# Modulation and expert steps of two 512 KB weight tiles instead of one, in a kernel whose TensorE order is planned ahead

## Chip, core and metric

The kernel runs on one core of a Trainium2 chip. The metric is the device time of one execution in microseconds; the smaller, the better. TensorE (PE in the profile) does the matrix products, VectorE (DVE), ScalarE (ACT) and GpSimd (POOL) the rest, and SyncE (SP) issues nearly all loads.

## What is computed

256 tokens of width 1024 go through two networks in turn. The first is one block: an RWKV-7 mixer run in both directions beside a gated linear attention, then a mixture of 32 experts with two experts per token. The second is two layers of an attention block that also carries 256 context tokens through the first layer and part of the second. Its layers are modulated by vectors that depend on two condition vectors alone (c and c_ctx):

```python
def first_block(x, ...):
    h = rmsnorm(x, ln1_w)
    p = h @ w_in
    mix = concatenate([rwkv7_mixer(p[..., :RWKV_COLS], ...), gla_mixer(p[..., RWKV_COLS:], ...)])
    x = x + mix @ w_out
    x = x + hier_moe(rmsnorm(x, ln2_w), ...)          # 32 experts, 2 per token
    return rmsnorm(x, ln_f_w)

def second_block(x, c, ctx, c_ctx, w_ada, ...):
    for l in range(2):
        ml = split(silu(c) @ w_ada[l] + b_ada[l], 9)       # modulation of the tokens
        mc = split(silu(c_ctx) @ w_ada[l] + b_ada[l], 9)   # modulation of the context
        # ffn, mixer over context and tokens, ffn; the same for the context, but for its last parts
```

All weights are float32. `silu(c) @ w_ada` is a product of two rows with a 1024 x 9216 matrix, so it is nearly all loading; the same holds for the experts, which see at most 32 tokens each in this stage.

## The kernel before

**Weights.** Every large weight comes in tiles of 128 x 1024 float32 (512 KB), which `raw` (L303) loads into one of 8 buffers (13 while the context's feed-forward parts have the pool "room" open). The dense layers split a tile into a high and a low part (L319 on ACT, L320 on DVE or POOL) and multiply with three products (`mm3`, L334 to L336). The modulation (`ada`, L1458) and the experts (`moe`, L1338 for gate and up, L1348 for down) multiply the raw tile directly. Their left operand has 32 columns, so each of a tile's four products goes to another 32 columns of the array; the trace shows a tile as 8 matmul instructions of the form 128*32. A layer's modulation has 72 tiles (144 in all), the experts have 256 tiles of gate and up and 128 of down, in 8 groups of four experts.

**Order.** The order of the instructions on PE and SP is the order in which the program issues them; nothing is reordered afterwards. Two generators issue it in turn, `first()` (mixers, then experts) and `second()` (modulation of both layers, then the context's way through the second network), and `_run` (L1993) picks between them by a model of time. At each `yield` a generator tells what the step cost on PE and how long its next step must wait for results. `raw` keeps a second clock, of when each tile will have arrived: 1.46 us per tile at best, and not before its buffer is free (`arrival`, L290).

One of the two generators counts as the *loading* task. `_run` lets it go ahead of the other when the next tile has, by the model, been there for `slack` us (I call the time by which model time is ahead of the arrival, the *lead*); otherwise the other goes first if it is ready. If only one is ready, it goes, whatever the lead.

- While the mixers run, the modulation is the loading task, slack is 2 us, and after each of its steps it must pause 0.5 us (`pace`). So a mixer step that is ready always comes between two steps of the modulation.
- While the experts run, they are the loading task and the context's feed-forward and mixer parts are the other. Slack is 8 us for the first four groups and 2 us for the rest, pace is 0. Here expert steps follow each other until the lead is below the slack.

**The mixers in the order of the trace.** Projections and gated linear attention (`products`, `shifted`, `gla`), 26 to 148 us; the start of `scoring` (head norms, decay), to 177; the loop over `items` in `scoring` with its steps of 5.2, 1.8 and 2.5 us (L839 to L853), to 259; `invert` (L862), a chain of 62 operations on DVE that runs to about 302, while `solve` (L886) waits and `beside` (L663) and the modulation fill PE; the inverse goes to memory and back (L935, L937); `solve` proper, a chain of small products (L916, L943, L962, L906) and copies (L928, L930), 316 to 373; `rwkv_out` and the output projection, to about 440. The experts' stretch is 462 to 1541 us. From there the context's rest and then the tokens run alone with no step that the change touches.

After every 16 tiles of a modulation (8 for the last), four groups of small DVE operations (L1465 to L1469) turn the sums into columns; after its last tile follow L1476, L1480 and `lam` (L1485).

Of the kernel before, what the change touches and what calls it, by code (L numbers as in the profile page):

```python
# [230 lines left out]
class _Net:  # L231
# [1063 lines left out]
    def moe(self, ch, x, load, loads):  # L1295

        nc = self.nc
        mm, V, A = nc.tensor.matmul, nc.vector, nc.scalar
        self.htok = ch.tile([128, 2, D], "htok")
        self.slot, self.wt = ch.tile([128, 2, 32], "slot"), ch.tile([128, 2, 32], "wt")  # L1300
        with ch.scope("rt") as cr:
            yield from self.route(cr, x)
        loads()
        for g in range(8):
            if g == 4:
                self.slack = 2.0
            s = ch.tile([128, 2, 4, 32], "ms")
            sw = ch.tile([128, 2, 4, 32], "msw")
            e = slice(4 * g, 4 * g + 4)
            for i in range(2):  # L1310
                V.tensor_tensor(s[:, i], self.c("iota")[:, None, :].to_broadcast([128, 4, 32]),
                                self.slot[:, i, e, None].to_broadcast([128, 4, 32]), op=OP.is_equal)
                V.tensor_tensor(sw[:, i], s[:, i], self.wt[:, i, e, None].to_broadcast([128, 4, 32]), op=OP.mult)
            xt = ch.tile([128, KD, 128], "mx")
            for q in range(2):
                b = ch.bank()
                for k in range(4):
                    for i in range(2):
                        kk = q * 4 + k
                        mm(b[:, k * 128:k * 128 + 128], self.htok[:, i, kk * 128:kk * 128 + 128],  # L1320
                           s[:, i].rearrange("p a b -> p (a b)"), start=(i == 0), stop=(i == 1))
                A.copy(xt[:, q * 4:q * 4 + 4].rearrange("p a b -> p (a b)"), b)
            st, ws = ch.tile([128, T], "mst", F32R), ch.tile([128, 1], "mws")
            b = ch.bank()
            for i in range(2):
                nc.tensor.transpose(b[:, i * 128:i * 128 + 128], s[:, i].rearrange("p a b -> p (a b)"), self.ident)
            for i in range(2):
                mm(b[:, T:T + 1], sw[:, i].rearrange("p a b -> p (a b)"), self.ones[:, :1], start=(i == 0), stop=(i == 1))
            V.tensor_copy(st, b[:, :T])
            V.tensor_copy(ws, b[:, T:T + 1])  # L1330
            yield 3.9, 0.6
            bg, bu = ch.bank(), ch.bank()
            for k in range(KD):
                for m, b in enumerate((bg, bu)):
                    for q in range(2):
                        r = load(self.d["moe_gu"][(g * KD + k) * 2 + m][:, q * 1024:q * 1024 + 1024])
                        for j in range(4):
                            mm(b[32 * j:32 * j + 32, q * 256:q * 256 + 256], xt[:, k, 32 * j:32 * j + 32],  # L1338
                               r[:, j * 256:j * 256 + 256], start=(k + q == 0), stop=(k == KD - 1), skip_group_check=True)
                        yield 0.45  # L1340
            ht = yield from self.swiglu_rows(ch, bg, bu, 128)
            bb = [ch.bank(), ch.bank()]
            for k in range(4):
                for n in range(2):
                    for q in range(2):
                        r = load(self.d["moe_dn"][(g * 4 + k) * 2 + n][:, q * 1024:q * 1024 + 1024])
                        for j in range(4):
                            mm(bb[n][32 * j:32 * j + 32, q * 256:q * 256 + 256], ht[:, k, 32 * j:32 * j + 32],  # L1348
                               r[:, j * 256:j * 256 + 256], start=(k + q == 0), stop=(k == 3), skip_group_check=True)
                        yield 0.45  # L1350
            y = [ch.tile([128, 2, 512], t, F32R) for t in ("mx", "myl")]
            for n in range(2):
                A.mul(y[0][:, n], bb[n], ws[:, 0:1])
                V.scalar_tensor_tensor(y[1][:, n], bb[n], ws[:, 0:1], y[0][:, n].bitcast(F32), op0=OP.mult, op1=OP.subtract)
            yield 0.0, 0.7
            for d in range(4):
                b = ch.bank()
                for i in range(2):
                    c = (2 * d + i) * 128
                    for n in range(2):  # L1360
                        mm(b[:, i * T:i * T + T], y[n][:, c // 512, c % 512:c % 512 + 128], st, start=(n == 0), stop=(n == 1))
                o = x[:, 2 * d:2 * d + 2].rearrange("p a b -> p (a b)")
                V.tensor_tensor(o, b, o, op=OP.add)
                yield 0.9
# [78 lines left out]
    def ada(self, ch, l):  # L1443

        nc = self.nc
        w = self.d[f"wada{l}"]
        if l == 0:
            yield 0.0, 5.0
        m2 = [self.cp.tile([128, 72], F32, name=f"mod{l}{m}") for m in range(2)]
        for s in range(5):  # L1450
            b = ch.bank()
            nb = 512 if s < 4 else 256
            for k in range(KD):
                for q in range(nb // 256):
                    m, o = (s * KD + k, q) if s < 4 else (4 * KD + k // 2, k % 2)
                    r = self.raw(w[m][:, o * 1024:o * 1024 + 1024])
                    for j in range(4):
                        nc.tensor.matmul(b[32 * j:32 * j + 32, q * 256:q * 256 + 256], self.cond[:, k],  # L1458
                                         r[:, j * 256:j * 256 + 256], start=(k + q == 0), stop=(k == KD - 1),
                                         skip_group_check=True)  # L1460
                    yield 0.45
            for q in range(nb // 128):
                t = ch.tile([128, 128], "adat", bufs=1)
                u = ch.tile([128, 128], "adau", bufs=1)
                nc.vector.tensor_copy(t, b[:, q * 128:q * 128 + 128])  # L1465
                nc.vector.transpose(u, t)
                c = slice(s * 16 + q * 4, s * 16 + q * 4 + 4)
                for m in range(2):
                    nc.vector.tensor_tensor(m2[m][:, c], u.rearrange("p (b c) -> p b c", c=32)[:, :, m],  # L1469
                                            self.v(f"b_ada{l}")[:, c], op=OP.add)  # L1470
        out = []
        for m in range(2):
            mm = m2[m].rearrange("p (n k) -> p n k", k=KD)
            a = self.cp.tile([128, 3, KD], F32, name=f"nsc{l}{m}")
            for i in range(3):
                nc.vector.scalar_tensor_tensor(a[:, i], mm[:, 3 * i + 1], 1.0, self.v(f"norm_g{l}{i}"),  # L1476
                                               op0=OP.add, op1=OP.mult)
            g = self.cp.tile([128, 3, KD], F32, name=f"gsc{l}{m}")
            for i in range(3):
                nc.vector.tensor_scalar(g[:, i], mm[:, 3 * i + 2], 0.5, None, op0=OP.mult)  # L1480
            out.append(dict(shift=[mm[:, 3 * i] for i in range(3)], scale=[a[:, i] for i in range(3)],
                            gate=[g[:, i] for i in range(3)]))
        return out
# [430 lines left out]
class _Stream:  # L1914
# [14 lines left out]
    def load(self, c):  # L1929
        if c not in self.raw:  # L1930
            o = (c % 2) * 1024
            self.raw[c] = self.net.raw(self.src[c // 2][:, o:o + 1024])
# [244 lines left out]
```

## Time and profile before

| | us |
|---|---|
| median of 3 runs | 2898.14 |
| range of the runs | 2897.85 to 2900.83 |
| the profiled execution: its own time | 2895.48 |
| its span, first to last instruction | 2893.7 |
| PE busy in it | 2763.3 |

The profiled execution is 1.8 us longer than its span, and 2.7 us below the median of the runs. A matmul's end is modelled in the profile, so a busy PE may still have gaps; how long a tile really holds PE is read from the starts of the instructions around it. "PEclk" is the clock granted to TensorE, 1.00 for 2.4 GHz and 0.50 for 1.2 GHz. The window views give for each stretch its length, the busy time of each engine with its number of instructions, PEclk, the share of the DMA engines that was busy and the rate of loading.

### The profile page before, as it was taken

To read this page: it belongs to the slowest core of one execution; us is meant where nothing else is said; L and a number is where in the kernel's file an instruction comes from. 1 tells how busy PE (TensorE), PEld (TensorE's weight loads), DVE (VectorE), ACT (ScalarE), POOL (GpSimd) and SP (SyncE) were. 2 spreads that over 40 slices of the span, in tenths; PEclk is the share of its full clock that TensorE was granted. 3 is DMA by queue.
4 is the path that set the end of the run, shared out by engine and by line. 5 is a ranking of instruction groups with operands and counts; after the bars stand their busy time and mean duration, and the time that the engine had idled before them with its cause. 6 is when DMAs were issued, how large, how long until landed. Compare 5 with 4: busy or idle time off the path is not lost. (4 is left out here: it accounts for less than half of the span.)

```text
span 2893.7 us, 59118 instructions
## 1 busy us (share of the span) xinstructions
PE 2763.3 (95%) x24442; PEld 2442.7 (84%) x24442; DVE 1780.1 (62%) x3517; ACT 1235.5 (43%) x2071; POOL 178.8 (6%) x207
## 2 busy tenths in 40 slices
PE   8998879999999999999997999999999999999999
PEld 6765568898667878888886999889999999899999
DVE  4766456455444655455456667767866767776865
ACT  4331133334243433334344445465544545365553
POOL 0110120000000100000001000100200000101100
PEclk9999979999999999999998999999999999999999
DMA  9857767987888888879794566424555565334563
GB/s 331 304 165 241 251 234 279 318 322 262 279 312 292 276 324 336 334 267 378 282 360 172 174 195 201 139 88 130 169 196 193 183 194 200 112 102 144 168 193 130
DMA packets 190849, 667.73 MB, mean 231 GB/s; under 512 B 28786, under 2 KB 29810, under 8 KB 189938
## 3 DMA queue, kind: packets, MB, share of 16 engines
q1 hardware_dynamic: 180144, 656.04, 65.6%
q10 hardware_dynamic: 10434, 7.90, 0.9%
q8 instruction: 192, 3.15, 0.4%
q14 instruction: 79, 0.65, 0.1%
HBM read 658.05 MB, written 5.80 MB: 229 GB/s over the span
## 5 line engine op out<-in xcount | busy, mean ns | idle before, releaser
L320 DVE TENSOR_TENSOR wlo<-raw,whi 128x1024 fp32r<-128x1024 f32 x625 | 769.6, 1233 | 491.4 <-ACT whi L319 480.1
L319 ACT CAST whi<-raw 128x1024 fp32r<-128x1024 f32 x633 | 663.8, 1050 | 775.9 <-issue 260.6
L334 PE MATMUL bz<-hnhz,whi 128*128 128x256 f32 x1920 | 540.6, 282 | 0.7 <-ACT hnhz L328 0.7
L335 PE MATMUL bz<-hnlz,whi 128*128 128x256 f32 x1920 | 533.4, 278 | 4.1 <-DVE hnlz L329 4.1
L336 PE MATMUL bz<-hnhz,wlo 128*128 128x256 f32 x1920 | 532.9, 278 | 1.9 <-DVE wlo L320 1.9
L334 PE MATMUL bc<-hnhc,whi 128*128 128x256 f32 x1504 | 435.1, 289 | 11.5 <-ACT whi L319 8.6
L336 PE MATMUL bc<-hnhc,wlo 128*128 128x256 f32 x1504 | 422.6, 281 | 6.3 <-DVE wlo L320 6.3
L335 PE MATMUL bc<-hnlc,whi 128*128 128x256 f32 x1504 | 423.1, 281 | 4.0 <-DVE hnlc L329 2.2
L334 PEld LDWEIGHTS bz<-hnhz,whi 128*128 128x128 f32 x1920 | 362.4, 189 | 9.6 <-issue 5.7
L335 PEld LDWEIGHTS bz<-hnlz,whi 128*128 128x128 f32 x1920 | 362.4, 189 | 5.5 <-DVE hnlz L329 5.4
L336 PEld LDWEIGHTS bz<-hnhz,wlo 128*128 128x128 f32 x1920 | 362.1, 189 | 2.1 <-DVE wlo L320 2.1
L334 PEld LDWEIGHTS bc<-hnhc,whi 128*128 128x128 f32 x1504 | 287.9, 191 | 51.6 <-issue 32.3
L336 PEld LDWEIGHTS bc<-hnhc,wlo 128*128 128x128 f32 x1504 | 286.6, 191 | 8.2 <-DVE wlo L320 8.2
L335 PEld LDWEIGHTS bc<-hnlc,whi 128*128 128x128 f32 x1504 | 287.4, 191 | 5.8 <-DVE hnlc L469 3.0
L336 PE MATMUL bz<-h0z,wlo 128*128 128x256 f32 x704 | 194.3, 276 | 0.0
L335 PE MATMUL bz<-h1z,whi 128*128 128x256 f32 x704 | 194.3, 276 | 0.0
L334 PE MATMUL bz<-h0z,whi 128*128 128x256 f32 x704 | 194.3, 276 | 0.0
L334 PE MATMUL bc<-h0c,whi 128*128 128x256 f32 x528 | 151.6, 287 | 0.0
L335 PE MATMUL bc<-h1c,whi 128*128 128x256 f32 x528 | 146.8, 278 | 0.0
L336 PE MATMUL bc<-h0c,wlo 128*128 128x256 f32 x528 | 146.7, 278 | 0.0
L320 DVE TENSOR_TENSOR wlo<-room,whi 128x1024 fp32r<-128x1024 f32 x73 | 89.5, 1226 | 73.0 <-ACT whi L319 65.8
L334 PEld LDWEIGHTS bz<-h0z,whi 128*128 128x128 f32 x704 | 132.2, 188 | 0.0
(702 smaller groups left out, 5235.3 us busy)
## 6 DMA issues: line engine op xcount, KB each, us to landing
raw<-wi SPq DMA_DIRECT2D x261, 512.0 KB, 4.8
raw<-moe_gu SPq DMA_DIRECT2D x191, 512.0 KB, 7.6
raw<-wada SPq DMA_DIRECT2D x144, 512.0 KB, 5.7
raw<-wo SPq DMA_DIRECT2D x128, 512.0 KB, 4.8
raw<-wbr SPq DMA_DIRECT2D x108, 512.0 KB, 3.8
raw<-win SPq DMA_DIRECT2D x104, 512.0 KB, 5.6
raw<-moe_dn SPq DMA_DIRECT2D x99, 512.0 KB, 6.9
room<-moe_gu SPq DMA_DIRECT2D x65, 512.0 KB, 8.5
```

The lines of the kernel that those rows point to most:

```text
L319: self.nc.scalar.copy(hi, src)
L320: eng.tensor_tensor(lo, src, hi.bitcast(F32), op=OP.subtract)
L334: mm(out, w[0], x[0], start=first, stop=False, **kw)
L335: mm(out, w[0], x[1], start=False, stop=False, **kw)
L336: mm(out, w[1], x[0], start=False, stop=last, **kw)
```

## The change

In `moe`, the `yield` after each tile of gate and up, and of down, moves out of the loop over q: one step now loads and multiplies two tiles in a row and tells 0.9 us where two steps told 0.45 us each. In `ada` it is the same for the first four parts (s < 4), where the two halves q of a 1 MB piece make one step; in the fifth part, which has one tile per k, the step ends after every second k. The products, the loads and their order within each generator stay as they are; what can change is how the two generators are interleaved.

```diff
@@ -1337,7 +1337,7 @@
                         for j in range(4):
                             mm(b[32 * j:32 * j + 32, q * 256:q * 256 + 256], xt[:, k, 32 * j:32 * j + 32],
                                r[:, j * 256:j * 256 + 256], start=(k + q == 0), stop=(k == KD - 1), skip_group_check=True)
-                        yield 0.45
+                    yield 0.9
             ht = yield from self.swiglu_rows(ch, bg, bu, 128)
             bb = [ch.bank(), ch.bank()]
             for k in range(4):
@@ -1347,7 +1347,7 @@
                         for j in range(4):
                             mm(bb[n][32 * j:32 * j + 32, q * 256:q * 256 + 256], ht[:, k, 32 * j:32 * j + 32],
                                r[:, j * 256:j * 256 + 256], start=(k + q == 0), stop=(k == 3), skip_group_check=True)
-                        yield 0.45
+                    yield 0.9
             y = [ch.tile([128, 2, 512], t, F32R) for t in ("mx", "myl")]
             for n in range(2):
                 A.mul(y[0][:, n], bb[n], ws[:, 0:1])
@@ -1458,7 +1458,8 @@
                         nc.tensor.matmul(b[32 * j:32 * j + 32, q * 256:q * 256 + 256], self.cond[:, k],
                                          r[:, j * 256:j * 256 + 256], start=(k + q == 0), stop=(k == KD - 1),
                                          skip_group_check=True)
-                    yield 0.45
+                if s < 4 or k % 2:
+                    yield 0.9
             for q in range(nb // 128):
                 t = ch.tile([128, 128], "adat", bufs=1)
                 u = ch.tile([128, 128], "adau", bufs=1)
```

## Rows read from the trace of the kernel before

**Rows 1.** The page's busy times over the span
```profile
PE 2763.3 (95%) x24442; PEld 2442.7 (84%) x24442; DVE 1780.1 (62%) x3517; ACT 1235.5 (43%) x2071; POOL 178.8 (6%) x207
```

**Rows 2.** Windows: length, PE, PEld, DVE, ACT, POOL (x instructions), PEclk, DMA share, GB/s
```profile
26.00:148.00 122.00, 119.94 (x1034) 89.92 (x1033) 72.80 (x176) 41.30 (x66) 14.07 (x36) 1.00 0.89 304
...
177.00:259.00 82.00, 80.41 (x600) 59.33 (x599) 53.15 (x169) 21.52 (x59) 8.83 (x12) 1.00 0.51 145
259.00:303.00 44.00, 35.42 (x316) 17.10 (x308) 33.45 (x95) 3.58 (x6) 4.90 (x2) 0.81 0.91 334
...
316.00:373.00 57.00, 53.12 (x1013) 38.19 (x1005) 20.23 (x52) 10.17 (x18) 2.37 (x1) 1.00 0.77 258
...
462.00:1032.00 570.00, 551.00 (x5066) 454.39 (x5069) 292.12 (x551) 215.26 (x376) 26.07 (x28) 0.99 0.83 291
1032.00:1541.00 509.00, 498.72 (x4874) 436.39 (x4862) 266.74 (x416) 193.75 (x274) 10.46 (x12) 0.99 0.88 328
270.00:280.00 10.00, 6.56 (x64) 1.43 (x64) 8.21 (x40) 0.00 (x0) 0.00 (x0) 0.76 1.03 408
```

**Rows 3.** Timeline of PE: a visit of one down tile, and one of two
```profile
1133.95 0.28 PE L335 MATMUL bc<-h1c,whi 128*128 128x256 f32 x1
1134.07 0.28 PE L336 MATMUL bc<-h0c,wlo 128*128 128x256 f32 x1
1134.28 0.64 PE L1348 MATMUL bm<-raw,mtm 128*32 128x256 f32 x8
1134.85 0.38 PE L334 MATMUL bc<-h0c,whi 128*128 128x256 f32 x1
...
1138.80 1.07 PE L1348 MATMUL bm<-raw,mtm 128*32 128x256 f32 x16
1139.80 0.38 PE L334 MATMUL bc<-h0c,whi 128*128 128x256 f32 x1
```

**Rows 4.** Waits of PE's weight loads, 462 to 1540 us: total, times, longest
```profile
PEld bc L334 <- issue: 54.5, 131, 0.8
...
PEld bm L1338 <- DMA raw<-moe_gu: 7.6, 6, 1.9
```

**Rows 5.** Windows of line 1458 alone on PE, columns as in rows 2
```profile
26.00:148.00 122.00, 28.75 (x360) 1.00 0.89 304
148.00:177.00 29.00, 7.33 (x80) 0.76 0.58 191
177.00:259.00 82.00, 13.80 (x176) 1.00 0.51 145
259.00:303.00 44.00, 21.30 (x248) 0.81 0.91 334
...
316.00:373.00 57.00, 15.01 (x192) 1.00 0.77 258
373.00:421.00 48.00, 10.53 (x104) 0.68 0.56 199
```

**Rows 6.** DVE by line, 270 to 303 us: count, busy us, mean ns, idle before
```profile
L879 DVE TENSOR_TENSOR kkx<-ldx 128x31 f32<-128x31 f32 (+15 forms) x31 | 12.7, 408 | 0.9
...
L1465 DVE COPY adata<-ba 128x128 f32<-128x128 f32 x4 | 1.1, 284 | 1.5 <-PE ba L1458 1.5
```

**Rows 7.** Timeline of all engines in the solve
```profile
324.34 0.64 PE L1458 MATMUL ba<-raw,cond 128*32 128x256 f32 x8
...
324.45 0.69 DVE L928 COPY xxx<-bx 32x512 f32<-32x512 f32 x1 [0.74 <-PE bx L962]
325.08 1.20 PE L916 MATMUL hx<-xxx,lqx 32*32 32x64 f32 x32
...
350.41 0.64 PE L1458 MATMUL ba<-raw,cond 128*32 128x256 f32 x8
...
350.98 1.08 PE L962 MATMUL bx<-xxx,ttx 32*32 32x64 f32 x32
```

**Rows 8.** DMA issues by line: the inverse read back, median us to landing
```profile
ttx<-scr ACTq DMA_DIRECT2D x2, 256.0 KB, 10.2
```

## Prediction

> **What bounds the kernel now.** I read the busy times first: PE is busy in 95% of the span, the next engine in 62% [rows 1]. Then the windows, since a mean over stages says little. The change touches two stretches, the mixers with the modulation (26 to about 421 us) and the experts with the context (462 to 1541 us), and the windows show two kinds of bound. In the experts' stretch, in the projections and in the scoring loop PE is busy in 97 to 98% of the time [rows 2]; time taken from PE there is time won. Around the inversion DVE is busy for 33 of 44 us and PE waits, and in the solve a chain of small products and copies runs, with PE holes that the modulation fills [rows 2, 5]. So the same tile costs its full time in one place and nothing in another, and the question is where the tiles go.
>
> **What a visit costs.** PE goes to the tiles and back to the split products. Between two such products it takes 0.12 us from start to start; a visit of one tile puts 1134.85 - 1134.07 = 0.78 us between them. From its first product to the return a visit of one tile takes 0.57 us, one of two 1.00 us [rows 3]. So a tile is 0.43 us, and a visit costs 0.78 - 0.12 - 0.43 = 0.23 us beyond its tiles. The waits show its larger part: after 131 such visits the weight load that follows has an "issue" gap of 54.5 us in all, 0.42 us each, some of which the tile's last products cover [rows 4]. The change removes no work; it can remove visits, at 0.23 us each.
>
> **Experts.** The timeline shows 177 visits for the 384 tiles, 69 of one tile and 75 of two (one of either kind stands in rows 3). How many are left follows from the planner's rule without a model of time: with pace 0, tile after tile goes when the lead is at or over the slack. If a step takes two, the pair goes where its first tile would have gone, since until then as many tiles are consumed as before. So a visit stays where it holds an odd-numbered tile of its part. Counting this in the timeline leaves 138: 107 become 75 before 1032 us and 70 become 63 after. In the second half most visits already hold two or three tiles, one per context step of 5.2 us, so there is little to merge.
> First half: 32 x 0.23 = 7.4 us, times the busy share of PE, 0.97, is 7 us. Second half: 7 x 0.23 = 1.6 us; there DMA is busy at 0.88 [rows 2], so I take 1 us. The second tile of a pair is wanted up to one visit earlier than now. The cover is the 8 us of slack in the first half; in the second the 2 us leave 2 - 1.46 + 0.45 = 1 us by the planner's own figures. If that cover fails, PE waits: today it waited 7.6 us in 6 places for gate and up tiles [rows 4]. Sum: -8 us, bounds -9 (all of it) and 0 (waits of the same size come back).
> A page of the Trainium skill speaks against it: DMA: Bandwidth & Descriptors, in Specifications, limits a core's loads from HBM to about 358 GB/s. By that the second half, at 328 GB/s, would be almost at the limit, and only the first half's 7 us would be won. The trace does not agree: a window of the modulation's loads reached 408 GB/s [rows 2], 1.28 us for 512 KB, so there is room.
>
> **Projections, 26 to 148 us.** Here the modulation takes one tile after every mixer step, 45 visits with 45 tiles [rows 5]; it never gets a second one because of the pause of 0.5 us. With two per step it may take more, until the lead is used up. From 53 us the mixer steps add up to about 69.6 us by the costs in their `yield`s (19 projections of 2.7 us, 18.3 us of linear attention), and load 19 tiles of 1.46 us; each modulation tile takes 1.46 - 0.45 = 1.01 us of lead. So 41.9 us / 1.01 = 42 tiles fit where 35 go now, and the 10 before stay: 52 tiles in 26 visits. Before 45 x 0.66 = 29.7 us, after 52 x 0.43 + 26 x 0.23 = 28.3 us: -1 us (bounds -5, if the tiles stay 45, and +2).
>
> **Start of the scoring, 148 to 177 us.** Ten tiles now [rows 5]; two per step make about 17. Seven more tiles are 3.0 us at 2.4 GHz and twice that at 1.2 GHz, and the mean clock is 0.76 here; holes of the head norm hide a part. +3 us (0 to 6).
>
> **Scoring loop, 177 to 259 us.** This is the term against the change. The steps are ready at once, so the planner alternates strictly: one mixer step, one modulation step, 22 visits of one tile [rows 5]. With DMA busy at 0.51 there is lead for two: a mixer step of 3.1 us and a pair make 4.0 us, against 2.9 us of loading. So there are still 22 visits, but 44 tiles, and 22 x 0.43 = 9.5 us more on a PE that is busy for 80.4 of 82 us: +9 us (bounds 0, if PE holes took all, and 9.5).
>
> **Inversion, 259 to 303 us.** By 259 us about 113 tiles are done instead of 77, the other 31 fit into the wait as 31 do now [rows 5], and the modulation is over before the solve. The price lies on DVE: its closing operations run inside the chain of 62 operations, which leaves DVE almost no idle time (0.9 us before 31 of them). One group of four (copy, transpose, two sums) is 0.28 + 0.30 + 2 x 0.15 = 0.9 us; four groups are inside now [rows 6]. After, I expect six, and the last 12 operations on columns and `lam`, about 20 of 0.15 to 0.2 us: +5 us (0 to 9). Then the inverse is written and read back, 10.2 us to landing, while modulation tiles are loaded [rows 8]; without them -2 us (-5 to 0; the lower end is an estimate, half of the landing time, if the two streams shared the engines evenly).
>
> **Solve and output, 316 to 421 us.** 22 visits leave the solve. Where PE waits for a copy anyhow, a visit is free: at 324.34 us it runs beside the copy of 0.69 us, and L916 starts when the copies are about done. At 350.41 us the next product waits for nothing else and starts 0.57 us later because of it [rows 7]. Following the copies through the timeline I find 15 of the 22 in the way: 15 x 0.6 = -9 us (0 to -14). In the output part 13 tiles in 5 visits lie mostly in waits at a clock of 0.68; their products and the DVE groups among the head norm's operations cost some us: -2.5 (-5 to 0).
>
> **Sum.** Mixers: -1 + 3 + 9 + 5 - 2 - 9 - 2.5 = +2.5 us; tiles that filled holes move to places without holes, and that eats what the solve gives back. Experts: -8. Together -5.5 us, against the profiled execution's own 2895.5 (span 2893.7) about 2890; the median of the runs lies 2.7 us higher, so **2893 us**. After 1541 us nothing changes, as the same products run in the same order.
>
> **Rivals.**
> (a) *The tiles stay where they are* and only visits fall away. The rule that I used for the experts, applied to the modulation, leaves 61 of 112 visits: 51 x 0.23 = 11.7 us, some 8 us of it where PE is the bound, with -8 of the experts: 2882 us. For it: DMA at 0.89 in the projections. Against it: DMA at 0.51 in the scoring loop [rows 2]. Chance 0.12.
> (b) *Slower: the clock falls in the solve.* There it is granted at 1.00 [rows 2], and beside the fills PE runs products of 32 x 32 with 64 columns and waits; without the fills the stretch resembles its neighbours, 259 to 303 at 0.81 and 373 to 421 at 0.68 [rows 2, 5]. PE's own work there is 53.1 - 15.0 = 38 us [rows 2, 5]. At 1.2 GHz for half of it, +15 us after waits shrink: 2908 us. It decides from about 10 us at the lower clock on, when it eats the gain. Against it: small products alone already run there between visits at the full clock. Chance 0.13. TensorE: Matmul & The Clock Gate of the Trainium skill (HAM oscillation) states the same mechanism, that waits between bursts of products put the array back to 1.2 GHz; by that the solve without fills would be slower, by the row of the solve it need not.
> (c) *The second tile comes late in the experts' stretch* and the 8 us return as waits for DMA: 2901 us. For it: 7.6 us of such waits today. Against it: 13 buffers and 408 GB/s. Chance 0.13.
>
> **How the numbers follow.** My sum has a chance of 0.62, with its terms between 2886 and 2900 us. A measurement of this kernel can tell about 0.2%, 5.8 us, from no change: faster is below 2892.3, slower above 2903.9. The sum lies close to the first line, so of its 0.62 I count 0.29 as faster, 0.31 as the same and 0.02 as slower; (a) is faster; (b) is slower with 0.12; (c) is the same with 0.09 and slower with 0.04. That makes 0.41, 0.41 and 0.18. The range takes in (a) in part, (c) and most of (b): 2884 to 2906.
>
> **What would show it.** Right: 44 tiles of the modulation between the start and the end of the scoring loop, which lasts some 9 us longer; none in the solve, which is some 9 us shorter at a clock of 1.00; about 138 expert visits and an "issue" sum of PE's weight loads down by a quarter. Wrong: modulation tiles still in the solve (a), PEclk below 0.9 there (b), waits of L1338 and L1348 for DMA well over 8 us (c).

## Result and the profile after

| | before | after |
|---|---|---|
| median of six runs, us | 2897.15 | 2921.81 |
| range, us | 2893.85 to 2900.83 | 2914.17 to 2930.77 |
| the profiled execution, span, us | 2893.7 | 2921.8 |

The change makes the kernel slower: the ratio is 1.0078, with a 95% interval of 1.0058 to 1.0099, some 25 us more, where the prediction's sum was 5.5 us less. PE's busy time hardly moved against [rows 1], 2769.1 us for 2763.3:

```profile
PE 2769.1 (95%) x24442; PEld 2478.2 (85%) x24442; DVE 1776.5 (61%) x3517; ACT 1233.7 (42%) x2071; POOL 176.1 (6%) x207
```

So the time went into PE's holes. Where they are, windows of the two stretches tell. First the projections, from 20 us to the first product of the scoring (L498), which came at 149.7 us before and comes at 157.9 now; then everything from the experts' first tile to the context's last product. The columns are those of [rows 2]; of each stretch the first fence is before, the second after.

```profile
20.00:149.70 129.70, 126.40 (x1084) 94.94 (x1083) 78.54 (x202) 43.03 (x69) 14.07 (x36) 1.00 0.89 307
```
```profile
20.00:157.90 137.90, 129.37 (x1145) 104.34 (x1144) 81.80 (x220) 42.99 (x69) 15.47 (x36) 0.95 0.88 318
```

```profile
465.20:1603.50 1138.30, 1090.07 (x10144) 923.34 (x10144) 600.64 (x1041) 433.58 (x698) 41.88 (x46) 0.98 0.83 301
```
```profile
484.50:1631.30 1146.80, 1086.06 (x10144) 934.72 (x10144) 597.91 (x1041) 431.84 (x698) 40.45 (x46) 0.98 0.81 298
```

In the projections PE is now without work for 8.5 us where it was for 3.3, and the clock is granted at 0.95 instead of 1.00. In the experts' stretch the same 10144 products take 4 us less of PE and leave 12.5 us more without work: 60.7 for 48.2 us. The waits of PE's weight loads as far as the last expert product show both sides. Each row gives the total in us, how often, and the longest; first two rows of before that [rows 4] leaves out, then after:

```profile
PEld bc L336 <- DVE wlo L320: 8.9, 10, 1.0
...
PEld bc L334 <- ACT whi L319: 6.3, 11, 1.3
```
```profile
PEld bc L334 <- issue: 37.1, 91, 0.4
PEld bc L336 <- DVE wlo L320: 18.8, 27, 1.0
PEld bc L334 <- ACT whi L319: 14.3, 15, 2.6
...
PEld bm L1338 <- DMA raw<-moe_gu: 6.1, 7, 1.9
```

The "issue" gaps behind visits fell from 54.5 [rows 4] to 37.1 us, as the forecast wanted. But the context's products now wait for the two parts of their split weights (L319, L320) for 33 us instead of 15. Waits for the experts' own tiles (moe_gu) did not grow. Behind the last expert product, where the rest of the context runs alone, the same waits are 7.8 us before (first fence) and 14.5 us after:

```profile
PEld bc L334 <- ACT whi L319: 7.0, 1, 7.0
...
PEld bc L336 <- DVE wlo L320: 0.8, 1, 0.8
```
```profile
PEld bc L334 <- ACT whi L319: 7.7, 1, 7.7
PEld bc L336 <- DVE wlo L320: 6.8, 2, 6.1
```

So of the 25 us by which they grew, 18 arose while the experts were still running, and 7 behind them. The modulation's tiles moved as forecast (line 1458 alone, as in [rows 5]; a tile has eight products):

```profile
26.00:157.90 131.90, 28.01 (x420) 10.85 (x416) 0.95 0.88 313
...
179.30:268.10 88.80, 20.40 (x308) 7.93 (x304) 1.00 0.78 255
268.10:318.00 49.90, 22.90 (x256) 6.84 (x256) 0.79 0.91 332
...
341.40:397.60 56.20, 0.06 (x4) 0.00 (x0) 0.70 0.05 18
```

The scoring loop, from the first to the last product of L794, took 38 tiles in 19 visits where it had taken 19 in 19, and the solve none. But the solve, 56.2 us from its first to its last product, ran at 0.70 where it had run at 1.00 [rows 2], and was 3.8 us longer instead of 9 us shorter. By this one profile rival (b) has come true, and four stretches are open as causes: projections, scoring loop, solve, experts.

### The profile page after: what moved, and what is told of

It is laid out like the page before. It is cut to its first block, busy times and chain, and to the rows that moved or that the text cites. A ratio compares the mean times of both kernels' runs of the same rounds, so it can differ in the third digit from the quotient of the medians.

```text
span 2921.8 us, 59133 instructions
## 1 busy us (share of the span) xinstructions
PE 2769.1 (95%) x24442; PEld 2478.2 (85%) x24442; DVE 1776.5 (61%) x3517; ACT 1233.7 (42%) x2071; POOL 176.1 (6%) x207
## 5 line engine op out<-in xcount | busy, mean ns | idle before, releaser
L320 DVE TENSOR_TENSOR wlo<-raw,whi 128x1024 fp32r<-128x1024 f32 x630 | 774.4, 1231 | 468.5 <-ACT whi L319 456.0
L319 ACT CAST whi<-raw 128x1024 fp32r<-128x1024 f32 x638 | 668.7, 1050 | 798.3 <-issue 261.7
L334 PE MATMUL bz<-hnhz,whi 128*128 128x256 f32 x1920 | 540.8, 282 | 0.7 <-ACT hnhz L328 0.7
L336 PE MATMUL bz<-hnhz,wlo 128*128 128x256 f32 x1920 | 533.2, 278 | 1.9 <-DVE wlo L320 1.9
L334 PE MATMUL bc<-hnhc,whi 128*128 128x256 f32 x1504 | 437.7, 291 | 16.9 <-DMA raw<-wi 7.5
L336 PE MATMUL bc<-hnhc,wlo 128*128 128x256 f32 x1504 | 428.2, 285 | 9.4 <-DVE wlo L320 9.2
L334 PEld LDWEIGHTS bz<-hnhz,whi 128*128 128x128 f32 x1920 | 362.7, 189 | 9.6 <-issue 5.7
L336 PEld LDWEIGHTS bz<-hnhz,wlo 128*128 128x128 f32 x1920 | 362.1, 189 | 2.1 <-DVE wlo L320 2.1
L334 PEld LDWEIGHTS bc<-hnhc,whi 128*128 128x128 f32 x1504 | 292.1, 194 | 48.5 <-issue 20.9
L336 PEld LDWEIGHTS bc<-hnhc,wlo 128*128 128x128 f32 x1504 | 290.3, 193 | 13.8 <-DVE wlo L320 13.6
L334 PE MATMUL bz<-h0z,whi 128*128 128x256 f32 x704 | 194.3, 276 | 0.0
L336 PE MATMUL bz<-h0z,wlo 128*128 128x256 f32 x704 | 194.3, 276 | 0.0
L336 PE MATMUL bc<-h0c,wlo 128*128 128x256 f32 x528 | 149.2, 283 | 7.7 <-DVE wlo L320 7.7
L334 PE MATMUL bc<-h0c,whi 128*128 128x256 f32 x528 | 152.1, 288 | 0.1
L336 PEld LDWEIGHTS bz<-h0z,wlo 128*128 128x128 f32 x704 | 132.2, 188 | 0.0
L334 PEld LDWEIGHTS bz<-h0z,whi 128*128 128x128 f32 x704 | 132.2, 188 | 0.0
```

What stands on the lines that cost most here:

```text
L319: self.nc.scalar.copy(hi, src)
L320: eng.tensor_tensor(lo, src, hi.bitcast(F32), op=OP.subtract)
L334: mm(out, w[0], x[0], start=first, stop=False, **kw)
L336: mm(out, w[1], x[0], start=False, stop=last, **kw)
```

## Experiments

Each time is a median of 4 to 11 runs, beside 18 to 30 runs of the kernel before on the same chip; the ratio is to those.

### Which half loses

e1 keeps the change in `ada` and puts the two places in `moe` back to steps of one tile, e2 the reverse. Against the kernel after:

```diff
e1, L1340 and L1350
-                    yield 0.9
+                        yield 0.45
e2, L1461
-                if s < 4 or k % 2:
-                    yield 0.9
+                    yield 0.45
```

> Modulation in pairs, experts tile by tile as before. In the changed kernel the experts begin 19.3 us later than before, and experts with the context's rest take 8.5 us more. Theory 1 (two separate causes, which add): the experts begin 19 us late and then take the 1138 us of before, so the time is about 2897 + 19 = 2916 us (2912 to 2920). Theory 2 (the modulation's pairs bring only a delay that later work makes up, and the loss is made in the experts): at most 2903 us. Theory 3 (only both together lose): within 5 us of 2897.

> Experts in pairs, modulation tile by tile as before. Theory 1: the experts begin where they did before (465 us), the weight-load gaps put down to issue fall by some 17 us, and waits for the split weights give it back, as in the changed kernel: 2897 + 8 = 2905 us (2900 to 2909). Rival (the forecast was right for the experts by themselves, and they lose in the changed kernel only because they begin later there): 2889 us (2885 to 2894).

Measured: e1 2903.29 us, ratio 1.0021 (1.0000 to 1.0042); e2 2909.68 us, ratio 1.0047 (1.0030 to 1.0065). Both halves lose, some 6 and 12 us; together 18, which the intervals allow to be the 25. The modulation's 6 is less than the 19 us by which the experts began late in the profile of after, and the total is 9 us below the range of e1's theory 1 and at the bound of its theory 2 (at most 2903 us: later work makes up for the delay). In e2 the experts begin 3 us later than in before (the first gather at 460.9 us for 457.6) and still lose 12 us, just above theory 1's range; so the rival there falls.

### The clock in the solve

e3 is the changed kernel with eight empty products behind L962 in each of the solve's eight steps (the line that hands over `ca` is left out here):

```diff
+                b = self.ca.bank()
+                for q in range(2):
+                    for j in range(4):
+                        mm(b[32 * j:32 * j + 32, q * 256:q * 256 + 256], self.cond[:, cc], self.vec[:, :256],
+                           start=True, stop=True, skip_group_check=True)
                 yield 0.8, 0.4
...
```

> The changed kernel, with eight empty products of a modulation tile's shape (128x32 weights, 256 columns, no load, a bank that nobody reads) behind the products with the inverse in each of the eight steps of the solve. They take the places that modulation tiles had in the kernel before. Theory 1 (the solve is slow because the tiles that kept TensorE at work between its small products are gone, and the clock falls): granted clock of the solve 0.9 or more where it is 0.67 to 0.79, first to last product of the solve 52 us where it is 56, time 2922 - 5 = 2917 us (2913 to 2919). Rival (the clock has another cause, so the fillers only cost their own time, 8 x 1 us less what the copies hide): clock unchanged, 2922 to 2930 us.

Measured: 2921.04 us, ratio 1.0082 (1.0055 to 1.0108), which is the changed kernel's own. The clock rose to 0.89, and the solve took 54.3 us instead of 56.2; in the total, which lies between the two forecasts, that isn't seen. The reason came out of the other runs: e2, e4 and e5 have the modulation, and with it the order of instructions as far as the experts, exactly as before. The solve in before, e2, e4, then in after, e3, and in e7 and e9 (both below; all tiles but 6 leave the solve there too), one window each from its first to its last product:

```profile
316.77:369.14 52.37, 49.54 (x963) 36.62 (x960) 17.64 (x45) 9.69 (x16) 2.37 (x1) 1.00 0.76 257
```
```profile
312.78:373.00 60.22, 57.49 (x963) 43.32 (x960) 17.65 (x45) 9.70 (x16) 2.34 (x1) 0.83 0.65 223
```
```profile
317.96:382.85 64.89, 61.20 (x964) 44.98 (x960) 17.66 (x45) 9.68 (x16) 2.36 (x1) 0.79 0.61 211
```
```profile
341.38:397.56 56.18, 51.63 (x813) 46.19 (x810) 17.05 (x36) 10.90 (x18) 6.61 (x3) 0.70 0.05 18
```
```profile
342.09:396.43 54.34, 50.48 (x942) 39.57 (x938) 16.20 (x36) 10.90 (x18) 4.78 (x2) 0.89 0.02 5
```
```profile
336.13:381.81 45.68, 41.81 (x861) 35.84 (x858) 17.48 (x36) 11.96 (x19) 7.12 (x3) 0.96 0.26 93
```
```profile
337.07:383.08 46.01, 42.15 (x862) 36.31 (x858) 17.54 (x36) 11.95 (x19) 7.22 (x3) 0.96 0.26 93
```

In before, e2 and e4 the same instructions run at 1.00, 0.83 or 0.79 of the clock and take 52 to 65 us. The profile of before was the fastest in the solve of nine executions that have 19 or 20 tiles there (52.4 to 64.9, mean 59.5 us), and that of after the slowest of five that have six or fewer and no empty products (after, e1, e7, e9, e12: 45.7 to 56.2, mean 48.9 us). Against the mean of the nine the solve gives back some 10.5 us in these five, and 6.7 us in the two that have no tile there at all, after and e1 (56.2 and 49.4 us). Rival (b) named a stretch where the clock does vary, but it varies with every tile in its place too, so one profile can't lay it to the tiles. Whether a solve without any tile runs slower on the whole stays open: after and e1 have 0.70 and 0.82, the three with four to six tiles 0.92 to 0.96, and those with 19 or 20 tiles 0.79 to 1.00.

### Experts: the visits or the place of the context

e4 and e5 are e2 with another margin (`slack`) for the planner: e4 with 9.5 and 3.5 us, e5 with 8.5 and 2.73 (shown).

```diff
-        net.slack, net.pace = 8.0, 0.0
+        net.slack, net.pace = 8.5, 0.0
-                self.slack = 2.0
+                self.slack = 2.73
```

> Modulation tile by tile, experts in pairs, and the margin by which the planner lets weight tiles wait before it prefers them to the context widened by one tile's time on the queue (8.0 to 9.5 in the first four groups, 2.0 to 3.5 in the last four). Theory 1 (the pairs let the experts run ahead of the context, whose rest then stands alone): the context is farther when the experts end, its rest behind the last expert product is below 90 us where the changed kernel has 131, and the time is 2889 us (2884 to 2895). Rival (the loss is in the split waits that pairs leave open wherever the experts stand): 2900 us or more, with the waits of the context's products for split weights still over 30 us.

> Experts in pairs, modulation as before, and the planner's margin set so that the context stands at each group of experts where it stood before the change (8.5 in the first four groups, 2.73 in the last four; by the planner's own count the context has done 614 and 711 us of its 820 at groups 6 and 7, as before, where pairs with the old margin have 588 and 656, and the wider margin of the last run 656 and 752). Theory 1 (a pair saves its visit, some 17 us in all, and the loss is only that the experts run ahead of the context): time from the first gather of the experts to the context's end 1146 - 10 = 1136 us, total 2897 - 9 = 2888 us (2883 to 2893). Rival (pairs leave the waits for split weights open wherever the context stands): 2900 us or more, with the context's three-pass products still 15 us or more above the 739 us of before.

Measured: e4 2916.30 us, ratio 1.0069 (1.0044 to 1.0094); e5 2900.44 us, ratio 0.9993 (0.9977 to 1.0009). The timelines tell how far the context is when the last expert product runs: 6613 of its 6826 products before, 6101 after and in e2, 6799 in e4, 6605 in e5. So with the old margin the experts run ahead, and 500 products more of the context stand alone at the end. The planner asks the margin for a pair's first tile alone, which would give such a lead; that this is the whole reason was not tested, only that the margin sets it. e4 overdid it: the tokens, which wait for the experts, began only at 1621.8 us, when the context's rest was over, where before they began 37 us ahead of its end. Its profile is 11 us longer than before's behind the context's end, and its profiled run had a slow solve too (64.9 us, above) and was the slowest of its four, so its time says little on the experts. The waits of PE's weight loads from the experts' first gather to the context's last product, in before, in e2 and then in e5:

```profile
PEld bc L334 <- ACT whi L319: 13.3, 12, 7.0
PEld bc L336 <- DVE wlo L320: 9.7, 11, 1.0
```

```profile
PEld bc L334 <- issue: 37.9, 93, 0.4
PEld bc L336 <- DVE wlo L320: 24.8, 28, 6.1
PEld bc L334 <- ACT whi L319: 23.1, 16, 7.7
```

```profile
PEld bc L334 <- issue: 46.8, 110, 2.0
PEld bc L334 <- ACT whi L319: 11.2, 11, 2.7
PEld bc L336 <- DVE wlo L320: 9.8, 13, 1.0
```

With the context level, the waits for split weights fall from 48 to 21 us, which is no more than the 23 of before. They do so with hardly more visits (5 on some 130). By the timelines, 11 of the 18 us by which they grow in e2 while the experts run lie between the context's products 1500 and 3500; there before has 85 visits and 6.9 us of such waits, e2 58 visits and 18.0 us, e5 55 visits and 9.0 us, and at the same product the experts of e2 are only 1 to 6 tiles farther than before. So what the margin sets is where the visits stand among the splits; their number isn't what opens the waits. The steps from one start of a PE instruction to the next in the same stretch, summed by what stands at both ends (visits: into, inside and out of the experts' tiles; three-pass: from one product of L334 to L336 to the next; rest: all others), in us:

```
            visits   three-pass   rest     sum
before        245        739       162    1146
e1            245        736       157    1138
after         228        767       160    1154
e2            227        767       159    1154
e5            225        749       159    1133
e12           225        753       162    1140
```

Pairs take 17 to 20 us out of the column of visits, and the column of three-pass products grows by 28 us, of which levelling recovers 14 to 18. A part of this only changes columns: where a visit no longer stands between two products of the context, the step of 0.12 us between them counts elsewhere (25 such steps more in three-pass and 25 in the rest, of 50 visits fewer). So the visits themselves are worth 50 x 0.23 = 11.5 us, an estimate by the forecast's price, and the three-pass products pay 25 us beyond those steps. The stretch took 1137.6 to 1146.0 us in eight executions without pairs (mean 1141), 1153.6 to 1154.5 in three with pairs, and 1133.2, 1141.7 and 1140.6 levelled (e5, e9, e12; mean 1138.5). So theory 1 is right that the margin takes away the loss, and too high on the gain: levelled pairs are worth some 2 us in the profiles and nothing that e5's interval can tell from zero, not 10, since 10 to 14 us (3 of them steps that changed columns) stay in the three-pass products, in places that were not traced further. The rival's time of 2900 us came true, without its mechanism: the three-pass products are 10 us above before, not 15, and the waits for split weights not above it.

### Modulation: which stage

e6 has pairs for the first 48 tiles alone (about the projections), e7 for all others alone; e8 has pairs throughout, with a pause (`pace`) of 2.5 us. The experts are as before in all three.

```diff
e6
+                    if l or s > 2:
+                        yield 0.45
-                if s < 4 or k % 2:
+                if l == 0 and s < 3:
                     yield 0.9
e7
+                    if l == 0 and s < 3:
+                        yield 0.45
-                if s < 4 or k % 2:
+                if (l or s > 2) and (s < 4 or k % 2):
                     yield 0.9
e8
-    net.slack, net.pace = 2.0, 0.5
+    net.slack, net.pace = 2.0, 2.5
```

> Pairs for the first 48 tiles of the modulation alone (the projections), tile by tile behind them; experts as before. Theory 1 (in the projections a pair covers one wait for a split weight where two single tiles covered two; three such waits of 1.6 to 3.2 us come open and the clock falls behind them): scoring begins 8 us late, time 2897 + 8 = 2905 us (2901 to 2908). Rival (what the projections lose, later stages give back, since the tiles taken early are not there later): 2897 us (2893 to 2900).

> The complement: the first 48 tiles one by one, pairs from there on; experts as before. Theory 1 (the scoring loop takes 19 tiles more, 9 us, the solve gives 8 to 9 back, as was forecast): 2897 us (2893 to 2901). Rival (the tiles missing in the solve cost there, by the clock, and what they take in the scoring loop is not given back): 2905 us or more.

> Modulation in pairs, experts as before, and the planner's pause behind a step of the modulation raised from 0.5 to 2.5 us, so that pairs come half as often as single tiles did: by the planner's list the scoring loop gets about 20 tiles where the changed kernel has 39 and the kernel before 20, and the solve keeps its own. Theory 1 (what was lost in the modulation is the place of the tiles, and visits by themselves save 0.2 us each): 2897 - 8 = 2889 us (2884 to 2894). Rival (half as many visits leave waits for split weights and small products open wherever they stand): 2900 us or more.

Measured: e6 2914.93 us, ratio 1.0048 (1.0025 to 1.0072); e7 2896.54 us, ratio 0.9979 (0.9963 to 0.9996); e8 2908.70 us, ratio 1.0016 (1.0001 to 1.0032). The loss comes with the pairs of the projections: 14 us by the median, of which their own stretch shows 7 (below); where the rest lies was not found. From the scoring on pairs gain 5 us, close to theory 1: loop longer, solve and output shorter. e8 came out as its rival said, at 2900 us or more, but not by its waits: the projections were shorter (48 tiles in 24 visits, scoring at 146.6 us). Its tiles lasted to 438 us, beyond the output projection, and from that projection's last product to the experts' first gather it took 46.6 us where it had taken 38.1; one profile shows this, and no run tested it.

### Projections: loads, products or number of tiles

e10 loads the first 48 tiles two by two and multiplies them one by one; e11 loads them one by one and multiplies two in a visit (e10 is e11 without the `yield 0.0` and with `yield 0.45` behind each tile); e13 is the kernel before with nine loads more, which nothing reads.

```diff
e11, behind the load of r
+                    held.append((q, r))
+                    if l == 0 and s < 3 and q == 0:
+                        yield 0.0
+                        continue
+                    for q, r in held:
...
-                    yield 0.45
+                    yield 0.9 if l == 0 and s < 3 else 0.45
+                    held = []
e13, ahead of the load of r
+                    if l == 0 and s < 3 and q == 0 and k % 3 == 0:
+                        x = self.rps[0][0].tile([128, 1024], F32, tag="raw", name="raw", bufs=8)
+                        self.nc.sync.dma_start(x, w[m][:, o * 1024:o * 1024 + 1024])
```

> The first 48 modulation tiles loaded two by two, their products still one tile at a time, at the places of the kernel before; the rest as before. In the projections' pairs alone 14 us were lost. Theory A (the loads do it: two modulation tiles stand before the projections' own weights in the load queue and its eight buffers): scoring begins 5 us or more late, 2905 to 2915 us. Theory B (the products do it: half as many visits cover half as many waits for split weights): scoring begins where it did before (149.7 us), 2900 us (2896 to 2903).

> The complement: the first 48 modulation tiles loaded one at a time, at the kernel before's pace, but the products of every two held back and done in one visit; the rest as before. Some 46 tiles then fall into the projections, as before, where pairs brought 54. Theory B (visits too few to cover the waits for split weights): scoring begins 5 us or more late, 2905 to 2915 us, with gaps of 1.5 to 3 us before products of the projections. Theory A (queue and buffers): 2900 us (2896 to 2903). Theory C (the 8 tiles more that pairs bring into the projections): both kernels of this pair near 2900 us.

> The kernel before, with nine loads of a modulation tile more in the projections (one ahead of every third step of the first 48 tiles' first half), which no product reads and the planner doesn't count. The changed kernel brought 8 tiles more into the projections and lost 8.2 us there, while the products of 46 tiles in pairs, brought one at a time, gained 4.1. Theory 1 (a tile too many costs there by its transfer, since the projections' own weights wait behind it): scoring begins 157 us or later where it is 149.7, with the waits for win's tiles longer, and the total is 2901 + 8 = 2909 us (2905 to 2914). Rival (transfers have room there, at a share of 0.89; the tiles cost by the order of their products): scoring within 2 us of 149.7, total 2898 to 2904 us.

Measured: e10 2904.37 us, ratio 1.0011 (0.9995 to 1.0028); e11 2888.76 us, ratio 0.9956 (0.9937 to 0.9976); e13 2907.18 us, ratio 1.0031 (1.0015 to 1.0046). From the timelines, up to the first product of the scoring (gaps of PE over 1 us):

```
            tiles     visits  scoring begins   gaps, us
before         46         46       149.7         none
after          54         27       157.9         1.6  3.0  3.2
e6             52         28       157.0         1.6  3.0  3.7
e10            45         45       150.2         1.0
e11            46         23       145.6         1.9
e13       46 + 9 unread   46       155.4         2.2  2.2
```

Half the visits with the same tiles gain 4.1 us (23 x 0.23 = 5.3 by the forecast's price), so theory B falls; loads two by two cost 0.5 us, so theory A falls. What costs is tiles beyond 46: six to nine of them put 6 to 8 us on the stretch, and nine do it by their loads alone (each with its place in the load queue and in the eight buffers), with 5.7 us (less than the 7 that e13's theory 1 asked for, more than the 2 of its rival). The other sign that theory 1 named did not come: ACT waits 18.8 us for win's tiles in e13 and 26.1 us in before, so that the loads cost is shown, and that they cost by late tiles of win is not. Theory C named the number of tiles, but both its kernels should have stayed at 2900 us; e11 is 12 us faster than before, three times what it gains up to the scoring, and the rest of that was not found. The windows of e11 and e13 to the same point, beside the two above:

```profile
20.00:145.60 125.60, 121.47 (x1081) 98.82 (x1080) 78.84 (x198) 42.51 (x69) 15.19 (x36) 0.99 0.88 312
```
```profile
20.00:155.40 135.40, 127.86 (x1078) 96.14 (x1077) 78.61 (x196) 42.35 (x69) 16.70 (x36) 0.99 0.91 328
```

PE's busy time falls by 4.9 us in e11, 0.21 us for each of the 23 visits. How a gap looks and what follows it, in the kernel after: the timeline of PE, the last steps of DVE ahead of it, and windows around it.

```profile
120.74 0.28 PE L335 MATMUL bx<-hnlx,whi 128*128 128x256 f32 x1
123.99 0.58 PE L336 MATMUL bx<-hnhx,wlo 128*128 128x256 f32 x1 [2.97 <-DVE wlo L320]
```
```profile
122.11 0.17 DVE L350 TENSOR_TENSOR rgtx<-rgtx,rgax 128x8 f32<-128x8 f32 x1
122.31 0.17 DVE L351 SCALAR_TENSOR_TENSOR rgyx<-rgtx,rgyx 128x8 f32<-128x8 f32 x1
122.51 0.29 DVE L449 TENSOR_SCALAR dgx<-const,rgyx 128x128 f32<-128x128 f32 x1
122.72 1.22 DVE L320 TENSOR_TENSOR wlo<-raw,whi 128x1024 fp32r<-128x1024 f32 x1
```
```profile
119.50:121.00 1.50, 1.50 (x19) 0.72 (x18) 1.27 (x8) 0.60 (x1) 0.10 (x1) 1.00 0.89 325
121.00:124.00 3.00, 0.03 (x2) 0.02 (x1) 2.73 (x11) 0.49 (x1) 0.00 (x0) 0.71 1.03 419
124.00:129.00 5.00, 5.00 (x23) 5.00 (x24) 1.26 (x2) 0.56 (x1) 0.00 (x0) 0.50 0.90 321
129.00:131.00 2.00, 2.00 (x19) 2.00 (x18) 1.78 (x6) 0.00 (x0) 0.61 (x1) 0.97 0.24 98
```

The low part of a weight (`wlo`) is in DVE's queue behind a chain of small operations, PE stands for 3.0 us, and the clock is at 0.50 for the 5 us behind, in which a product starts every 0.21 us, where it is 0.12 at the full clock [rows 3]. TensorE: Matmul & The Clock Gate of the Trainium skill (HAM oscillation) says that waits between bursts of products put the array back to the lower clock; the last rows agree, with 1.00 ahead of the gap and 0.50 behind it. Which of a tile's loads delays which split, step by step, was not followed; that the loads alone open gaps is shown by e13 (2.2 and 2.2 us).

### The pieces that gain, together

e9 is e7 with e5's experts; e12 has e11's first 48 tiles besides.

```diff
+                    if l == 0 and s < 3:
+                        yield 0.45
-                if s < 4 or k % 2:
+                if (l or s > 2) and (s < 4 or k % 2):
                     yield 0.9
```

> The two pieces that did not lose, together: modulation tile by tile for its first 48 tiles and in pairs from there on, experts in pairs with the margin that keeps the context level (8.5 and 2.73). Theory 1 (the gains add: -4.6 us for the later pairs, about -3 for the level experts in the means): 2900 - 8 = 2892 us (2886 to 2896), the first version below the kernel before. Rival (the two use the same slack, since fewer tiles are left for the solve and the context starts elsewhere): 2897 us or more.

> The three pieces together: the first 48 modulation tiles loaded one at a time with products in pairs, later modulation pairs as in the change, experts in pairs with the margin that keeps the context level. Theory 1 (the pieces act in different stages and add: -12.8 us for the first, -10.7 for the other two): scoring begins 4 us earlier than before, 2901 - 23 = 2878 us (2872 to 2884). Rival (the plan of the stages behind shifts with the first and eats part of it): 2885 to 2893 us.

Measured: e9 2891.55 us, ratio 0.9963 (0.9948 to 0.9978); e12 2888.52 us, ratio 0.9969 (0.9952 to 0.9986). Both beat the kernel before, and so does e11 alone, by some 9 to 13 us. The pieces of e9 add up. e12 has the early scoring of e11 (4.7 us), and in the profiles its experts begin 5.1 us before those of e9, but its ratio is no better; its time lies in the rival's range, and whether that gain is lost behind or drowned in the scatter stays open.

## Why the prediction was wrong

The stages by the timelines, in us, from one product's start to another's: the loop goes from the first to the last product of L794, the solve as in the windows above, the output to the last product of its projection, routing to the experts' first gather. "Profiles" is after less before. Since the clock varies, the last column has means over executions of the same kind (single tiles: before, e2, e4, e5, and e13 from the scoring on; pairs as in the change: after, e1, e3).

```
stage                          forecast   profiles   over executions
projections                       -1        +8.2     +8 (157.8 to 157.9; 149.5 to 150.0)
scoring to experts               +3.5      +11.0     +3 (317.3; 314.4)
  start                           +3        -1.7
  loop                            +9       +10.4
  inverse to first solve product  +3        +7.7
  solve                           -9        +3.8     -7 (52.8, after and e1; 59.5, nine executions)
  output                         -2.5      -14.0
  routing                          0        +4.8
experts and context               -8        +8.5    +13 (1154; 1141)
```

The last column adds up to 24 us, about the measured loss. Its +3 is uncertain by as much again, since the executions with single tiles lie between 307.9 and 324.2 us.

**Visits and most places were right.** In the scoring loop every visit took two tiles, as forecast: 38 tiles in 19 visits (the forecast's 44 in 22 were counted in a longer window), for 10.4 us where 9 were forecast; none in the solve; 127 expert visits where 138 were forecast. The price of 0.23 us a visit holds: e11 saved 0.21. Between scoring and experts the terms missed singly, the output by 11.5 us, and that their sum came near, 3.5 forecast and 2.9 measured, is luck. The solve's term of -9 fits the -7 of the two without tiles and the -13 of the three with four to six (46.3 us); one profile of each kernel made it look wrong.

**Projections: the step that failed is "52 tiles in 26 visits".** The count was nearly right, 54 in 27, and so was PE's time for the tiles themselves, 28.0 us for 28.3 forecast. But the tiles beyond 46 were priced by their 0.43 us of PE alone. In a stretch with PE at 98% and DMA at 0.89 [rows 2] their loads alone cost 5.7 us (e13). In the kernel after, PE, which had stood for 3.3 us in all, stood for 8.5, most of it in three gaps before low parts that came late on DVE, and its busy time grew by 3.0 us at a clock of 0.95. The loads' cost and these gaps were put at nothing, and for the upper bound of +2 no reason is given. How a load delays a split stays open.

**Experts: the step that failed is the cover, with its bound of 0.** The forecast took the margin as cover for loads alone and asked whether the experts' own tiles would come late, rival (c). They did not: 7.6 us of waits before [rows 4], 6.1 after. It never asked what becomes of the other generator's waits, those of the context's products for their split weights, which grew from 23 to 48 us. The bound "0, waits of the same size come back" excluded a loss without a reason. The runs show that the margin decides: with 8.5 and 2.73 us instead of 8 and 2, and as few visits, these waits are 21 us and the loss is gone (e5). That a visit in the right place covers the time in which ACT and DVE make the next split is the likely reason; it is argued from the waits, and no run shows it step by step. It isn't mainly the context's last part standing alone, since only 7 of the 25 us arise there. The visits were worth some 11.5 us where 9 were the most that was counted, because 50 fell away and not 39.

**Rivals.** (a) Of the kernels with modulation pairs, tiles stayed in the solve in e6, e8 and e11, and e11 shows its worth: faster by 12 us, of which 4 are found. (b) the clock of the solve did differ, but it does so with all tiles in place; whether a solve without any is slower for it stays open. (c) fell on its mechanism, though something of its size came in its place. None named what decided: in the projections the loads of the tiles beyond 46, in the experts' stretch the context's waits for its splits. And the range, 2884 to 2906, did not reach the times of (a) and (b), 2882 and 2908, though it was said to take them in at least in part.

## What to carry to other kernels

Before merging the steps of a filler, ask how many of its tiles will then come, and what waits will open for the other stream: in the projections, with PE at 98% and DMA at 0.89, six to nine tiles too many cost 6 to 8 us, and nine loads without any product 5.7. Where a planner interleaves two streams by a margin, set the margin anew when a step's size changes, and compare how far each stream is at the same landmark; here that alone took away the 12 us lost in the experts. And compare a stage's time over several executions of the same order before a cause is sought in one profile.

## What the runs showed of the hardware that was not expected

The solve, with its 32 x 32 products, ran the same instructions at 1.00, 0.83 or 0.79 of the clock in different executions, 52 to 65 us. The scoring loop, too, took 78.5 to 79.6 us in six executions and 87.8 in e10 and e6 with the same 19 tiles, at clocks of 0.92 and 0.94, though one profile of each can't tell a draw from an effect of those kernels. A single PE gap of 3.0 us was followed by 5 us at 0.50. And taking 45 visits out of a stretch in which PE was busy for 96% of the time, some 10 us by their price, moved its end by only 2 to 3 us on the mean (e5, e9, e12), even with the margin set anew.
